# New state and output of a DeltaNet chunk: one shared PSUM bank, or one each

## The chip, the cores and the metric

The kernel runs on one core of a Trainium2 chip. A core has five engines, each with its own queue of instructions that it takes in order: TensorE (PE in the profile; its weight loads are PEld), VectorE (DVE), ScalarE (ACT), GpSimd (POOL) and SyncE (SP, which issues most DMAs here). They meet only at semaphores. TensorE writes its results into PSUM, which is divided into banks; VectorE and ScalarE read them from there. The metric is the device time of one launch in microseconds (us).

## What is computed

Two decoder layers on 1024 tokens of width 1024. Layer 0 mixes tokens with a gated DeltaNet (8 heads of 128), layer 1 with latent attention; each is followed by a dense SwiGLU network, and a conditioning vector sets shift, scale and gate of every part. The change is in the DeltaNet's recurrence, which in the reference is this scan over chunks of a head:

```python
def step(S, xs):
    q_i, k_i, w_i, u_i, a_i, gl_i = xs
    v_new = u_i - jnp.einsum("bhck,bhkv->bhcv", w_i, S)
    o_i = jnp.einsum("bhck,bhkv->bhcv", q_i, S) + jnp.einsum("bhij,bhjv->bhiv", a_i, v_new)
    S = S * gl_i[..., None, None] + jnp.einsum("bhck,bhcv->bhkv", k_i, v_new)
    return S, o_i
```

The state S (128 x 128 per head) is all that passes from one chunk to the next. The kernel takes chunks of 128 tokens, so a head has 8 (c = 0 to 7).

## The kernel before

The DeltaNet stage goes through the 8 heads one after the other (`gdn_heads`). Work of three kinds is laced into one order for TensorE: the recurrence of head h, the preparation of heads h + 1 and h + 2 (convolved keys, queries and values, decay matrices, the triangular inverse), and a stream F of projection matmuls, 128 x 512 each, for the heads to come (`take(F, n)` lets n of them go; n is 12 for heads 0 to 4, 9, 8 and 10 for heads 5, 6 and 7). In head 7 F is the output projection.

TensorE's order in this stage is the one written down. VectorE, ScalarE, GpSimd and SyncE get theirs from a scheduler, which places each instruction when it expects its inputs.

One chunk of the recurrence, by the lines of the kernel before:

- part 0: two matmuls on the state, K S (L535) and Q S (L536), into one tile `pks`. VectorE makes r from the first (L538), ScalarE makes qs from the second (L541). Then 12 matmuls of F.
- part 1: the matmul on r with the inverse U (L545); ScalarE copies it out as y (L547). Then `gdn_kv` transposes the next chunk's v and k (L515, L517) into one tile, and ScalarE reads them out as vs and kdr (L518, L522). Then, by chunk, pieces of the inverse (`gdn_merge`), L585, `gdn_kk` and `gdn_qq`.
- part 2: a tile `po` of two halves. The state's matmul (L552) fills the first half; VectorE updates S from it (L556; in chunk 0 a copy, L554). The output's matmul (L558) fills the second half; VectorE adds qs and keeps the result as `on` (L563; in chunk 0 a copy, L565). ScalarE squares and sums `on` (L567). Chunk 7 has no state update. Then pieces of `gdn_at` and `gdn_L`, 12 more matmuls of F, and the next chunk.

All these tiles have the name "d" and come from the pool `pd`, which has two buffers, one bank each, used in turn:

```python
self.pd = s2.enter_context(tc.tile_pool(name="pd", bufs=2, space=PSUM))
```

A tile may be written when all readers of the tile before it in the same bank are done. With four tiles a chunk (pks, py, the transposes, po), pks and the transposes are always in one bank, py and po in the other. The other PSUM pools are `pp` (F), `pc` (tag "c") and `pe` (tag "e"), two buffers each, eight in all.

VectorE also runs the triangular inverse of a head ahead (L454 and L456 in turn, 31 times, then L459; L470 puts it into U), the convolution (L323, three times per half; L327), weight splits (L178), the sums for the conditioning vector (L117, L119), the diagonal of K K (L391) with its scale (L393 to L401) and the matrix L (L410). ScalarE's L326 is the tanh of the convolution and waits for the third L323. The small powers `rk` and `co` are GpSimd's (L219).

Of the kernel before, what the change touches and what calls it, by code (L numbers as in the profile page):

```python
# [9 lines left out]
F32 = mybir.dt.float32  # L10
# [4 lines left out]
ALU = mybir.AluOpType  # L15
# [4 lines left out]
P = 128  # L20
# [12 lines left out]
class Trunk:  # L33
# [491 lines left out]
    def gdn_rec(self, h, c, part):  # L525

        nc, v, kq, pr = self.nc, self.nc.vector, self.kqv[h], self.pr[h]
        g, cs, cc = h * NT + c, slice(c * P, (c + 1) * P), c % 4
        if part == 0:
            self.r, self.qs = self.kv[1], None  # L530
            if c == 0:
                self.S = self.gs.tile([P, P], F32, name="S")
                return
            pks = self.pd.tile([P, 2, P], F32, name="d")
            nc.tensor.matmul(pks[:, 0], kq["KT"][:, cs], self.S, start=True, stop=True)  # L535
            nc.tensor.matmul(pks[:, 1], kq["QT"][:, cs], self.S, start=True, stop=True)  # L536
            r = self.gw.tile([P, P], F32, name="r", bufs=2)
            v.scalar_tensor_tensor(out=r, in0=pks[:, 0], scalar=pr["c2"][:, c:c + 1], in1=self.kv[1],  # L538
                                   op0=ALU.mult, op1=ALU.add)
            self.qs = self.gw.tile([P, P], F32, name="qs", bufs=2)  # L540
            nc.scalar.activation(out=self.qs, in_=pks[:, 1], func=AF.Copy, scale=self.eg[:, g:g + 1])  # L541
            self.r = r
        elif part == 1:
            py = self.pd.tile([P, P], F32, name="d")
            nc.tensor.matmul(py, pr["U"][:, c], self.r, start=True, stop=True)  # L545
            self.y = self.gw.tile([P, P], F32, name="y", bufs=2)
            nc.scalar.copy(self.y, py)  # L547
            self.kd = self.kv[0]
        else:
            po = self.pd.tile([P, 2, P], F32, name="d")  # L550
            if c < NT - 1:
                nc.tensor.matmul(po[:, 0], self.kd, self.y, start=True, stop=True)  # L552
                if c == 0:
                    v.tensor_copy(self.S, po[:, 0])  # L554
                else:
                    v.scalar_tensor_tensor(out=self.S, in0=self.S, scalar=self.egl[:, g:g + 1], in1=po[:, 0],  # L556
                                           op0=ALU.mult, op1=ALU.add)
            nc.tensor.matmul(po[:, 1], pr["at"][:, c], self.y, start=True, stop=True)  # L558
            if cc == 0:
                pr["on"] = self.gw.tile([P, 4, P], F32, name="on"), self.gs.tile([P, 4], F32, name="ss")  # L560
            on, ss = pr["on"]
            if c > 0:
                v.tensor_tensor(out=on[:, cc], in0=po[:, 1], in1=self.qs, op=ALU.add)  # L563
            else:
                v.tensor_copy(on[:, cc], po[:, 1])  # L565
            junk = self.gw.tile([P, P], BF16, name="junk2")
            nc.scalar.activation(out=junk, in_=on[:, cc], func=AF.Square, accum_out=ss[:, cc:cc + 1])  # L567
            if cc == 3:

                t1 = self.gs.tile([P, 4], F32, name="t1")  # L570
                v.tensor_scalar(out=t1, in0=pr["qq"][:, c - 3:c + 1], scalar1=EPS, scalar2=P * EPS, op0=ALU.add,
                                op1=ALU.mult)
                v.scalar_tensor_tensor(out=t1, in0=ss, scalar=1.0 / P, in1=t1, op0=ALU.mult, op1=ALU.add)
                co = self.gs.tile([P, 4], F32, name="co")
                self.rpow(co, t1)
                v.tensor_tensor(out=on, in0=on, in1=co.rearrange("p (c o) -> p c o", o=1).broadcast_to([P, 4, P]),
                                op=ALU.mult)
# [1082 lines left out]
```

## Time and profile before

| | us |
|---|---|
| median of 3 timed runs | 2702.81 (2699.43 to 2705.99) |
| the profiled execution | 2703.33 |
| its span, first to last instruction | 2701.6 |
| TensorE busy (94% of the span) | 2531.3 |
| VectorE busy (73%) | 1979.5 |
| ScalarE busy (43%) | 1171.4 |
| GpSimd busy (6%) | 154.6 |
| mean granted TensorE clock | 0.973 of full speed |

A row of the order of time gives the start, the length, the engine, the line, what is written from what, and in brackets how long the engine stood idle before it and which instruction ended that. x2 means that two instructions are merged: a fp32 matmul of this kernel runs as two. A row of the table of stretches gives for each engine the busy time and the number of instructions, then the granted clock (1.00 is full speed). The ends of matmuls are modelled, and two matmuls overlap, so a sum of TensorE's lengths is more than its time.

### The profile page before, as it was taken

How to read it: one execution, taken by the hardware profiler on the slowest of the kernel's cores; microseconds unless marked ns; L12 is line 12 of the kernel's file. 1: busy time of each engine (PE TensorE's matmuls, PEld its weight loads, DVE VectorE, ACT ScalarE, POOL GpSimd, SP SyncE). 2: the span in 40 equal slices, each digit the busy share in tenths (PEclk: the TensorE clock that was granted, in tenths of full speed). 3: DMA queues.
4: the chain of work that ended last, by engine and by line, in shares of the span. 5: the costliest groups of instructions: out<-in, count | busy, mean ns of one | idle time of the engine just before them, and what ended most of it. 6: DMA issues, size and time to landing. Idle time of an engine off the chain costs nothing.

```text
span 2701.6 us, 35351 instructions
## 1 busy us (share of the span) xinstructions
PE 2531.3 (94%) x12749; PEld 2095.8 (78%) x12749; DVE 1979.5 (73%) x3748; ACT 1171.4 (43%) x2366; POOL 154.6 (6%) x322
## 2 busy tenths in 40 slices
PE   6968898888889999999999999999989999999998
PEld 5657777776767888888888788888868888887776
DVE  5797888876755988878567866667658777774678
ACT  5535445454436523222234475555455333322443
POOL 1111111111000000000000010000000000000000
PEclk8989999999989999999999999999999999999999
DMA  6101221221155455544583622111563323325734
GB/s 221 40 24 36 79 83 56 86 82 40 40 169 194 145 164 175 165 140 160 179 293 94 216 85 65 49 46 59 170 205 100 102 97 108 103 94 198 250 101 140
DMA packets 258703, 327.60 MB, mean 121 GB/s; under 512 B 17578, under 2 KB 176448, under 8 KB 258528
## 3 DMA queue, kind: packets, MB, share of 16 engines
q1 hardware_dynamic: 235840, 284.37, 33.6%
q10 hardware_dynamic: 22688, 40.97, 4.0%
q8 instruction: 100, 1.64, 0.3%
q14 instruction: 75, 0.61, 0.1%
HBM read 247.16 MB, written 78.14 MB: 120 GB/s over the span
## 4 chain that ended last, share of the span: by engine, by line
PE 74%; DVE 14%; ACT 4%; DMA 4%; POOL 2%; issue 2%; SPq 0%; POOLq 0%; DVEq 0%; ACTq 0%
PE pd L1123 15%; PE nrm_p L202 14%; PE pd L202 9%; PE pj L202 7%; PE P L202 7%; PE pj L346 5%; PE pd L1440 3%; PE po L202 2%; DVE cacc L323 2%; PE pj L862 2%; DMA wraw<-in_ada_w_dram 2%; PE pq L202 1%; DVE X L456 1%; DVE st L454 1%; PE tp L1483 1%
## 5 line engine op out<-in xcount | busy, mean ns | idle before, releaser
L1123 PE MATMUL pd<-wlo,gh 128*128 128x512 f32 x616 | 244.1, 397 | 1.4 <-DVE wlo L178 1.0
L1123 PE MATMUL pd<-whi,gl 128*128 128x512 f32 x616 | 241.4, 393 | 1.0 <-DVE gl L178 1.0
L1123 PE MATMUL pd<-whi,gh 128*128 128x512 f32 x616 | 237.6, 395 | 3.6 <-ACT gh L177 3.3
L346 PE MATMUL pj<-hThi,whi 128*128 128x512 f32 x480 | 203.9, 425 | 0.0
L346 PE MATMUL pj<-hThi,wlo 128*128 128x512 f32 x480 | 196.5, 409 | 0.0
L346 PE MATMUL pj<-hTlo,whi 128*128 128x512 f32 x480 | 195.5, 407 | 0.0
L177 ACT CAST gh<-wraw 128x1024 fp32r<-128x1024 f32 x84 | 82.3, 979 | 247.0 <-PE pd L1123 207.8
L177 ACT CAST whi<-wraw 128x1024 fp32r<-128x1024 f32 (+3 forms) x105 | 100.8, 961 | 160.5 <-DMA wraw<-in_ffn_w_gate_dram 49.0
L1123 PEld LDWEIGHTS pd<-wlo,gh 128*128 128x128 f32 x616 | 116.5, 189 | 32.3 <-DVE wlo L178 6.9
L1123 PEld LDWEIGHTS pd<-whi,gh 128*128 128x128 f32 x616 | 116.6, 189 | 30.8 <-ACT gh L177 4.5
L178 DVE TENSOR_TENSOR gl<-wraw,gh 128x1024 fp32r<-128x1024 f32 x84 | 95.2, 1133 | 60.9 <-ACT gh L177 60.7
L1123 PEld LDWEIGHTS pd<-whi,gl 128*128 128x128 f32 x616 | 116.5, 189 | 27.0 <-DVE gl L178 1.4
L178 DVE TENSOR_TENSOR wlo<-wraw,whi 128x1024 fp32r<-128x1024 f32 (+3 forms) x105 | 116.3, 1108 | 27.7 <-ACT whi L177 26.3
L202 PE MATMUL nrm_p<-T,xrow 128*128 128x512 f32 (+1 forms) x576 | 133.7, 386 | 0.0
L202 PE MATMUL nrm_p<-T,ow_hi 128*128 128x512 f32 (+1 forms) x600 | 132.0, 368 | 0.0
L219 POOL TENSOR_TENSOR nrm_r<-nrm_r,mh 128x1 f32<-128x1 f32 x56 | 37.7, 674 | 1598.5 <-DVE nrm_r L213 1589.5
L202 PE MATMUL nrm_p<-T,ow_lo 128*128 128x512 f32 (+1 forms) x552 | 125.9, 376 | 0.0
L202 PEld LDWEIGHTS nrm_p<-T,xrow 128*128 128x128 f32 x576 | 105.1, 188 | 23.7
L202 PEld LDWEIGHTS nrm_p<-T,ow_hi 128*128 128x128 f32 x600 | 103.6, 188 | 20.7
L323 DVE SCALAR_TENSOR_TENSOR cacc<-cr,cwc,cacc 128x512 f32<-128x512 f32 x144 | 107.5, 753 | 12.9 <-ACT cacc L321 11.3
L202 PEld LDWEIGHTS nrm_p<-T,ow_lo 128*128 128x128 f32 x552 | 97.9, 188 | 20.6
L346 PEld LDWEIGHTS pj<-hThi,wlo 128*128 128x128 f32 x480 | 94.8, 197 | 21.5
(544 smaller groups left out, 6405.7 us busy)
## 6 DMA issues: line engine op xcount, KB each, us to landing
wraw<-in_ada_w_dram SPq DMA_DIRECT2D x80, 512.0 KB, 4.1
wraw<-in_ffn_w_gate_dram SPq DMA_DIRECT2D x44, 512.0 KB, 4.2
wraw<-in_ffn_w_up_dram SPq DMA_DIRECT2D x44, 512.0 KB, 4.7
gd_S<-sx ACTq DMA_DIRECT2D x88, 256.0 KB, 2.6
B<-in_ffn_w_down_dram SPq DMA_DIRECT2D x40, 512.0 KB, 6.9
wraw<-gd_S SPq DMA_DIRECT2D x40, 512.0 KB, 4.6
gd_A<-co ACTq DMA_DIRECT2D x66, 256.0 KB, 2.2
wraw<-in_gdn_w_in_dram SPq DMA_DIRECT2D x32, 512.0 KB, 4.2
```

The source lines that it names most:

```text
L177: nc.scalar.copy(hi, raw)
L178: nc.vector.tensor_tensor(out=lo, in0=raw, in1=hi.bitcast(F32), op=ALU.subtract)
L202: nc.tensor.matmul(out, l, r, start=(i == 0), stop=(i == len(seq) - 1))
L219: self.nc.gpsimd.tensor_tensor(out=out, in0=in_, in1=self.mh[:, 0:in_.shape[1]], op=ALU.pow)
L323: nc.vector.scalar_tensor_tensor(out=acc, in0=cr[:, j:j + 512], scalar=self.cw[:, j, ch:ch + 1], in1=acc, op0=ALU.mult, op1=ALU.add)
L346: self.nc.tensor.matmul(pj, l[:, kt], r[:, kt, sl], start=(kt == j == 0), stop=(kt == KT - 1 and j == 2))
L454: v.tensor_tensor(out=t[:, 0:n], in0=Lr[:, j, j + 1:32].rearrange("p (i o) -> p i o", o=1).broadcast_to([P, n, 8]), in1=X[:, j:j + 1].broa ...
L456: v.tensor_tensor(out=X[:, j + 1:32], in0=X[:, j + 1:32], in1=t[:, 0:n], op=ALU.subtract)
L862: nc.tensor.matmul(po, l[:, i], r[:, ns], start=(i == j == 0), stop=(i == 3 and j == 2))
L1123: nc.tensor.matmul(acc[t], x[:, j, ts], y[:, j], start=(j0 + j == 0 and k == 0), stop=(j0 + j == NJ - 1 and k == 2))
L1440: nc.tensor.matmul(sc[:, 0:nm], q[:, ts], k[:, cs], start=(i == 0), stop=(i == 4 and not last))
L1483: nc.tensor.transpose(pt[:, kt - k0], pes[qi][:, kt * P:(kt + 1) * P], self.ident)
```

## The change

The tile `po` of two halves becomes two tiles of 128 columns. `psn`, for the new state, is taken only in chunks 0 to 6; `po`, for the output, in every chunk. Both come from the same pool of two banks, so a chunk now takes five tiles instead of four: pks, py, the transposes, psn, po. Each chunk therefore starts on the other bank than the one before it, psn lies in the bank of py, and po in the bank of the transposes. The arithmetic and the number of instructions are the same. All lines from 558 on have a number higher by one.

```diff
--- before.py
+++ after.py
@@ -547,22 +547,23 @@
             nc.scalar.copy(self.y, py)
             self.kd = self.kv[0]
         else:
-            po = self.pd.tile([P, 2, P], F32, name="d")
             if c < NT - 1:
-                nc.tensor.matmul(po[:, 0], self.kd, self.y, start=True, stop=True)
+                psn = self.pd.tile([P, P], F32, name="d")
+                nc.tensor.matmul(psn, self.kd, self.y, start=True, stop=True)
                 if c == 0:
-                    v.tensor_copy(self.S, po[:, 0])
+                    v.tensor_copy(self.S, psn)
                 else:
-                    v.scalar_tensor_tensor(out=self.S, in0=self.S, scalar=self.egl[:, g:g + 1], in1=po[:, 0],
+                    v.scalar_tensor_tensor(out=self.S, in0=self.S, scalar=self.egl[:, g:g + 1], in1=psn,
                                            op0=ALU.mult, op1=ALU.add)
-            nc.tensor.matmul(po[:, 1], pr["at"][:, c], self.y, start=True, stop=True)
+            po = self.pd.tile([P, P], F32, name="d")
+            nc.tensor.matmul(po, pr["at"][:, c], self.y, start=True, stop=True)
             if cc == 0:
                 pr["on"] = self.gw.tile([P, 4, P], F32, name="on"), self.gs.tile([P, 4], F32, name="ss")
             on, ss = pr["on"]
             if c > 0:
-                v.tensor_tensor(out=on[:, cc], in0=po[:, 1], in1=self.qs, op=ALU.add)
+                v.tensor_tensor(out=on[:, cc], in0=po, in1=self.qs, op=ALU.add)
             else:
-                v.tensor_copy(on[:, cc], po[:, 1])
+                v.tensor_copy(on[:, cc], po)
             junk = self.gw.tile([P, P], BF16, name="junk2")
             nc.scalar.activation(out=junk, in_=on[:, cc], func=AF.Square, accum_out=ss[:, cc:cc + 1])
             if cc == 3:
```

TensorE has the same instructions in the same order; what differs is which engine's semaphore a matmul waits for. The rows are from head 6, chunk 6, where no matmul of F lies between the chunks. Names in brackets are the engines waited for.

Before:

```order
L496 MATMUL e<-U,L 64x64 [waits PE_49]
L496 MATMUL e<-U,L 64x64 x3
L498 MATMUL e<-ident,U 64x64 [waits PE_49]
L498 MATMUL e<-ident,U 64x64 x3
L552 MATMUL d<-y,kdr 128x128 [waits Activation_49]
L558 MATMUL d<-y,at 128x128 [waits DVE_49]
L535 MATMUL d<-S,KT 128x128 [waits Activation_49]
L536 MATMUL d<-S,QT 128x128
L545 MATMUL d<-r,U 128x128 [waits DVE_49]
```

Now:

```order
L496 MATMUL e<-U,L 64x64 [waits PE_49]
L496 MATMUL e<-U,L 64x64 x3
L498 MATMUL e<-ident,U 64x64 [waits PE_49]
L498 MATMUL e<-ident,U 64x64 x3
L552 MATMUL d<-y,kdr 128x128 [waits Activation_49]
L559 MATMUL d<-y,at 128x128 [waits Activation_49]
L535 MATMUL d<-S,KT 128x128 [waits DVE_49]
L536 MATMUL d<-S,QT 128x128
L545 MATMUL d<-r,U 128x128 [waits DVE_49]
```

The output's matmul (L558, now L559) waited for VectorE and waits for ScalarE now; the first matmul on the state (L535) waited for ScalarE and waits for VectorE now. So it is in every chunk.

VectorE's order, from the state's update of head 2, chunk 3, into chunk 4 (junk is the diagonal of K K, t and co the output's norm, b and c scales).

Before:

```order
L556 SCALAR_TENSOR_TENSOR S<-S,eg_947,d 128x128
L391 SCALAR_TENSOR_TENSOR junk,kd<-c,ident 128x128 x2
L563 TENSOR_TENSOR on<-d,qs 128x128
L391 SCALAR_TENSOR_TENSOR junk,kd<-c,ident 128x128
L393 TENSOR_SCALAR kd<-kd 128x4
L398 TENSOR_TENSOR rkb<-rk,beta 128x4
L573 SCALAR_TENSOR_TENSOR t_3715<-ss,t_3715 128x4
L400 TENSOR_TENSOR b_3705<-rk,rkb 128x4
L119 SCALAR_TENSOR_TENSOR wraw<-wraw,cact 128x1024
L401 SCALAR_TENSOR_TENSOR c_3685<-b_3705,eg_947 128x4
L576 TENSOR_TENSOR on<-on,co 128x512
L410 SCALAR_TENSOR_TENSOR L<-c,b_3705,dec 128x128 x4
```

Now:

```order
L556 SCALAR_TENSOR_TENSOR S<-S,eg_947,d 128x128
L391 SCALAR_TENSOR_TENSOR junk,kd<-c,ident 128x128
L564 TENSOR_TENSOR on<-d,qs 128x128
L391 SCALAR_TENSOR_TENSOR junk,kd<-c,ident 128x128 x2
L574 SCALAR_TENSOR_TENSOR t_3733<-ss,t_3733 128x4
L393 TENSOR_SCALAR kd<-kd 128x4
L577 TENSOR_TENSOR on<-on,co 128x512
L398 TENSOR_TENSOR rkb<-rk,beta 128x4
L538 SCALAR_TENSOR_TENSOR r<-d,c_1971,vs 128x128
L400 TENSOR_TENSOR b_3722<-rk,rkb 128x4
L178 TENSOR_TENSOR wlo<-wraw,whi 128x1024
L401 SCALAR_TENSOR_TENSOR c_3702<-b_3722,eg_947 128x4
```

r (L538) came right behind the L410 of the first list and now stands ahead of them; the step L119 has gone elsewhere; `on` stands one place nearer to S. In most chunks `on` follows S at once now.

ScalarE's order in head 1, chunk 1.

Before:

```order
L541 ACTIVATE qs<-d,eg_947 128x128
L547 COPY y<-d 128x128
L518 ACTIVATE vs<-d,rkb 128x128
L522 ACTIVATE kdr<-d,eg_947 128x128
L326 ACTIVATE KT<-cacc 128x512
L367 ACTIVATE decT<-c 128x512
```

Now:

```order
L541 ACTIVATE qs<-d,eg_947 128x128
L547 COPY y<-d 128x128
L518 ACTIVATE vs<-d,rkb 128x128
L326 ACTIVATE KT<-cacc 128x512
L522 ACTIVATE kdr<-d,eg_947 128x128
L367 ACTIVATE decT<-c 128x512
```

The tanh L326 has moved ahead of kdr. In chunk 1 of heads 0, 2, 3 and 4 it stood ahead of vs and now stands between vs and kdr.

## Rows read from the trace of the kernel before

**Rows 1.** The page's first line.

```profile
span 2701.6 us, 35351 instructions
```

**Rows 2.** Stretches: range, length, busy PE, PEld, DVE, ACT, POOL, clock, DMA share, GB/s.

```profile
194.64:266.87 72.23, 64.53 (x366) 54.03 (x366) 53.25 (x137) 37.23 (x101) 9.88 (x19) 0.98 0.10 31
266.87:611.14 344.27, 306.78 (x1675) 255.71 (x1673) 280.71 (x708) 166.52 (x441) 49.57 (x80) 0.95 0.26 77
611.14:813.50 202.36, 173.89 (x935) 143.48 (x934) 127.17 (x318) 85.09 (x239) 19.05 (x27) 0.92 0.26 85
sum 618.86, PE 545.20 PEld 453.22 DVE 461.13 ACT 288.84 POOL 78.49; mean PE 181.73 PEld 151.07 DVE 153.71 ACT 96.28 POOL 26.16
```

**Rows 3.** Waits of PE, 190 to 815 us: total us, times, longest.

```profile
PE d L558 <- DVE S L556: 50.6, 48, 2.2
PE d L558 <- DVE S L554: 7.7, 8, 1.2
...
PE d L545 <- DVE r L538: 3.1, 6, 0.9
```

**Rows 4.** Order of time, head 2, chunk 5.

```profile
416.62 0.49 PE L552 MATMUL d<-y,kdr 128*128 128x128 f32 x2
416.86 0.36 ACT L522 ACTIVATE kdr<-d,eg 128x128 f32<-128x128 f32 x1
...
418.11 0.57 DVE L488 TENSOR_SCALAR U<-e 32x128 f32<-32x128 f32 x2
...
418.72 0.35 DVE L556 SCALAR_TENSOR_TENSOR S<-S,eg,d 128x128 f32<-128x128 f32 x1
...
419.12 0.49 PE L558 MATMUL d<-y,at 128*128 128x128 f32 x2 [2.00 <-DVE S L556]
```

**Rows 5.** Order of time, head 2, chunk 2.

```profile
382.81 0.36 ACT L522 ACTIVATE kdr<-d,eg 128x128 f32<-128x128 f32 x1
...
383.39 0.49 PE L552 MATMUL d<-y,kdr 128*128 128x128 f32 x2
...
383.91 0.35 DVE L556 SCALAR_TENSOR_TENSOR S<-S,eg,d 128x128 f32<-128x128 f32 x1 [0.20 <-PE d L552]
...
384.31 0.49 PE L558 MATMUL d<-y,at 128*128 128x128 f32 x2 [0.44 <-DVE S L556]
...
384.84 0.29 DVE L563 TENSOR_TENSOR on<-d,qs 128x128 f32<-128x128 f32 x1
```

**Rows 6.** Chain that ended last: two runs of F behind head 2's chunk 5.

```profile
419.61 4.35 PE pj L346 x12
424.40 2.76 PE pj L346 x12
```

**Rows 7.** Order of time, head 0, chunk 1.

```profile
203.59 0.44 PE L552 MATMUL d<-y,kdr 128*128 128x128 f32 x2
204.05 0.63 ACT L326 ACTIVATE KT<-cacc 128x512 f32<-128x512 f32 x1 [1.05 <-DVE cacc L323]
...
204.84 0.36 ACT L522 ACTIVATE kdr<-d,eg 128x128 f32<-128x128 f32 x1
```

**Rows 8.** Order of time, head 1, chunk 4: the matmul on r.

```profile
317.96 0.49 PE L545 MATMUL d<-r,U 128*128 128x128 f32 x2 [0.17 <-DVE r L538]
```

**Rows 9.** Order of time, chunk 3: first and last of six, heads 0 and 5.

```profile
225.50 0.49 PE L558 MATMUL d<-y,at 128*128 128x128 f32 x2 [0.44 <-DVE S L556]
...
652.26 0.49 PE L558 MATMUL d<-y,at 128*128 128x128 f32 x2 [0.51 <-DVE S L556]
```

**Rows 10.** Stretches: chunk 1 of heads 0, 1, 3, 5, 6, the sum.

```profile
sum 60.92, PE 48.63 PEld 39.52 DVE 54.85 ACT 21.62 POOL 13.22; mean PE 9.73 PEld 7.90 DVE 10.97 ACT 4.32 POOL 2.64
```

**Rows 11.** Stretch of 2 us behind head 2's chunk 5, columns as in rows 2.

```profile
420.00:422.00 2.00, 2.00 (x7) 1.61 (x6) 1.97 (x6) 1.38 (x7) 0.00 (x0) 0.58 0.00 0
```

**Rows 12.** Waits of PE in heads 1 to 4, 266.87 to 611.14 us.

```profile
PE d L558 <- DVE S L556: 28.9, 24, 2.2
PE d L558 <- DVE S L554: 4.3, 4, 1.2
```

## The prediction

> **What bounds the kernel now.** I read the page first: the profiled execution spans 2701.6 us [rows 1] and took 2703.33 us, so 1.7 us lie around the span; the median of the three timed runs, 2702.81 us, is half a microsecond less. TensorE is busy most of the span, so only idle time of TensorE or a slow TensorE clock can be won anywhere. Second, the view by stretches, cut at the output matmuls (L558) of each head's last chunk: the recurrence that the change touches runs from 194.64 to 813.50 us. In its 618.9 us TensorE is busy 545.2 and VectorE 461.1 [rows 2], so TensorE idles 73.7 us, a ninth of the stage, while VectorE is not full either (75%; 82% in heads 1 to 4). Third, TensorE's waits of that stage: two rows, both L558 waiting for VectorE's write of the state S (L556, and L554 in chunk 0), hold 50.6 + 7.7 = 58.3 us in 56 waits, four fifths of the idle time; the wait for r (L545) is 3.1 us [rows 3].
>
> The order of time then shows why. In head 2, chunk 5, the state's matmul L552 starts at 416.62; VectorE is still in older work (L488 until 418.68), does S at 418.72, and only at 419.12 does L558 start, 2.00 us idle behind it [rows 4]. L558 needs y, which L552 had already, and not S. It waits because S's update reads the bank that L558 writes. Where VectorE is free at once, as in head 2, chunk 2, the wait is still 0.44 us [rows 5]. So the least is 0.44 and the mean 58.3 / 56 = 1.04 us.
>
> **What the change removes.** The output gets a tile of its own, so L558 waits for ScalarE alone and the wait for S moves to the next chunk's first matmul (L535), as the instruction orders show. Between the two stand 12 matmuls of the projection stream (9, 8 and 10 in heads 5 to 7), some 2.76 us [rows 6]. S ends 2.45 us after L552 in rows 4, one of the longest waits, and L535 cannot come before 0.49 + 0.3 + 2.76 = 3.5 us after it; only where the stream has run out (head 6, chunks 6 and 7) does nothing lie between. I count the wait at L535 as hidden, and if that cover were gone the 0.44 us least of rows 5 would come back. Removed: **58.3 us**.
>
> **What it adds, in five terms.**
>
> (a) A new wait. The ring of two banks now turns five times a chunk, and the output lands in the bank of the next chunk's transposed k and v, whose readers are ScalarE's vs and kdr (L518, L522). In rows 5's chunk kdr was done at 383.17, before L552; in chunk 5 kdr ends at 416.86 + 0.36 = 417.22, against 417.11 for the end of L552 [rows 4], a wait of 0.1 to 0.2. I take that for chunks 5 and 7, 14 in all: 2 us. In head 0, chunk 1, the tanh L326 stands ahead of kdr and waits for VectorE's convolution; kdr ends at 205.20, L552 at 204.03 [rows 7]: 1.2 us. Head 1 gets that order too. Together 2 + 2 x 1.2, rounded up to 5; bounds 0 and 12 (2.0 us, as in rows 4, in chunk 1 of five heads, and the 2). Queued behind the waiting L558 is the stream, and nothing but `on` waits for L558 itself.
>
> (b) r becomes late. VectorE does not become faster, so where it was behind, its next result is late next. In chunk 4 of head 1, the matmul on r (L545) already waits 0.17 us for it [rows 8]: no slack is left. What is saved at S in chunk 3 (0.44 in head 0 to 0.51 in head 5, six waits of heads 0 to 5, 6.8 in sum [rows 9]) and in chunk 0 (7.7 [rows 3]) can thus come back as a wait for r. Bounds: 0, since the new VectorE order puts r ahead of the four L410 and of a step for the conditioning vector (L119), and 14.5. I take the middle, 7.
>
> (c) Chunks in which VectorE has more to do than TensorE. In chunk 1 of heads 0, 1, 3, 5 and 6 VectorE is busy 54.85 us, TensorE 48.63 [rows 10]; without the wait these five are paced by VectorE, so 6.2 us stay, taken as 6. Bounds 0 (the new order spreads the substitution steps of L454 and L456 into chunks 2 and 3) and 12 (they then crowd those chunks as well).
>
> (d) VectorE's `on` (L563) now stands right behind S. It cannot start before L558 has run: L558 starts 0.49 after L552 at the earliest, `on` followed L558 by 0.53, so 1.02 after L552, while S ends 0.87 after it [rows 5]. VectorE idles 0.15 x 56 = 8.4 us, hidden in its 158 us of idle time. Bounds 0 and 8; I take 2.
>
> (e) TensorE's clock. After the 2.00 us wait of chunk 5 the granted clock fell to 0.58 of full in the stretch 420 to 422 [rows 11], that is, to the lower of its two levels (1.2 GHz) for most of it, and the next 12 stream matmuls took 4.35 instead of 2.76 us [rows 6]. It fell so in chunk 5 or 6 of each of heads 0 to 4. With the wait of chunk 5 cut to 0.2 us I expect those five falls gone: 5 x 1.59 = 8 us back. Bounds: 0, and 14 (nine falls that come within 2 us of a wait for S of 1.4 us or more).
>
> The Trainium skill's page "TensorE: Matmul & The Clock Gate", section "A second HAM failure mode: psum-queue depth-cycling", says that small idles between groups of matmuls that cycle through PSUM banks are enough to make the clock swing; the fall in rows 11 behind a 2 us wait agrees. Taken as the rule for the whole stage it would give back every slow stretch, which is the third rival below.
>
> Sum: -58.3 + 5 + 7 + 6 + 2 - 8 = -46.3 us. On the profiled execution's own 2703.3 us that is **2657 us**, all of it inside the recurrence (619 to some 573 us). The rest keeps its instructions: TensorE's order is the same to the last row, and only VectorE's, ScalarE's, GpSimdE's and SyncE's move, within this stage.
>
> **Rivals.**
> 1. VectorE takes over the pace in heads 1 to 4, where it is busy 280.7 of 344.3 us [rows 2]; the work it used to do between S and `on` now queues elsewhere, and TensorE waits for r instead of S. Then those heads keep most of their 344 us and only heads 0 and 5 to 7 gain, by their own waits for S (58.3 less the 33.2 of heads 1 to 4 [rows 12] is 25, some 20 after (a)): 2683. Half of it gives 2670. For it: [rows 8, 10]. Against it: VectorE idles 63 us in these heads, much of it waiting for TensorE.
> 2. Slower: kdr. ScalarE's tanh (L326) or its copies before kdr make L558 wait for kdr in every chunk as long as in rows 7, 1.2 us. 56 x 1.2 = 67 instead of 58.3, with the 2 us of chunk 7: 2714. It decides from a mean lateness of 1.04 us on. For it: the new ScalarE order puts L326 between vs and kdr in chunk 1 of several heads, and VectorE now stands still behind `on` while L558 waits, which delays the very convolution that L326 needs. Against it: in chunks like that of rows 5 kdr is done before L552 starts.
> 3. The clock comes back whole and VectorE keeps up: terms (b) to (d) fall away and some 25 us of TensorE's time at the lower level return (the stage's granted clock is 0.92 to 0.98, which costs 2% of 72 + 5% of 344 + 8% of 202 = 35 us [rows 2]; 10 of it lie in heads 6 and 7 behind other waits). -58.3 + 5 - 25 = -78: 2625. By the Trainium skill's section above this is the case to expect.
> 4. The change doesn't do what it says: the bank was not what held L558, or the chain through VectorE sets each chunk's length and L535 or L545 waits for all that L558 waited: 2703. Against it: in chunks like that of rows 5 VectorE itself had waited 0.20 us for TensorE before S, so there the chain runs through TensorE.
>
> **How the numbers follow.** Chances: forecast 0.52 (2645 to 2668), VectorE's pace 0.24 (2668 to 2692), the clock 0.10 (2620 to 2645), nothing 0.06, slower 0.08. A measurement of this kernel can tell 0.2%, 5.4 us, from no change. Faster is 0.52 + 0.24 + 0.10 = 0.86, same 0.06, slower 0.08. The best ends of the terms give 2703 - 58 - 14 = 2631, the worst with the clock unchanged 2703 - 58 + 12 + 14 + 12 + 8 = 2691. The range 2634 to 2690 leaves out a little of the third rival and the last two.
>
> **What the profile after would show.** Right: L559 (L558 before) waits for no VectorE instruction, and for ScalarE under 8 us in all; TensorE's idle time between the same marks falls from 74 to some 30 us; L545's wait for r grows from 3 to about 10 us; VectorE's share rises to about 80%; the falls of the clock behind chunk 5 are gone. (a) is wrong if the wait for kdr is over 12 us, (b) and (c) if the wait for r is over 20, (e) if the stage's granted clock does not rise. The whole is wrong if the stage shortens by less than 15 us, or if the time outside it moves by more than 5.

## The result and the profile after

The changed kernel takes 2635.27 us in the median of four runs (2630.46 to 2645.68), the kernel before 2701.12 beside it: a ratio of 0.976, with a 95% interval from 0.9724 to 0.9796. Forecast were 2657 us in a range from 2634 to 2690. The gain is 66 us and not 46. The measured time lies inside the range, 1.3 us from its lower end, and in the band of the third rival (2620 to 2645, chance 0.10), not in the forecast's own (2645 to 2668, 0.52).

The profiled execution is 72 us shorter than that of [rows 1]; the page counts the same work on each engine as before (12749 matmuls, 3748 instructions on VectorE, 2366 on ScalarE). First line of the page:

```profile
span 2629.7 us, 35337 instructions
```

The same three stretches as in [rows 2], cut at the output matmuls (now L559) of the same chunks:

```profile
195.41:259.56 64.15, 61.83 (x368) 52.49 (x366) 50.88 (x138) 38.06 (x102) 10.03 (x19) 1.00 0.13 37
259.56:560.74 301.18, 287.84 (x1674) 241.92 (x1672) 266.08 (x700) 167.51 (x441) 49.31 (x80) 0.99 0.30 88
560.74:742.01 181.27, 165.84 (x935) 137.88 (x933) 127.59 (x328) 85.74 (x239) 20.13 (x27) 0.94 0.29 95
sum 546.60, PE 515.50 PEld 432.28 DVE 444.54 ACT 291.30 POOL 79.47; mean PE 171.84 PEld 144.09 DVE 148.18 ACT 97.10 POOL 26.49
```

There are three readings. The stage went from 618.86 to 546.60 us, and the time outside it stayed (2082.7 before, 2083.1 now). TensorE's idle time (stretch less PE) went from 73.7 to 31.1. And TensorE's own busy time went from 545.2 to 515.5 with the same instructions, mostly because the granted clock rose from 0.98, 0.95 and 0.92 to 1.00, 0.99 and 0.94. A reader who looks at idle time alone misses the third reading, and it is nearly 30 of the 72 us.

The waits of TensorE (total us, times, longest), in answer to [rows 3]:

```profile
PE d L515 <- ACT qs L541: 9.6, 8, 2.7
PE d L545 <- DVE r L538: 6.5, 9, 2.2
PE d L559 <- ACT kdr L522: 3.6, 6, 1.6
PE c L586 <- DVE on L577: 2.7, 2, 1.8
...
PE d L535 <- DVE S L556: 0.2, 1, 0.2
```

The two waits for S are gone, and no other took their size. Head 2, chunk 5 again, in order of time, in answer to [rows 4]:

```profile
389.86 0.36 ACT L522 ACTIVATE kdr<-d,eg 128x128 f32<-128x128 f32 x1
...
390.68 0.39 PE L552 MATMUL d<-y,kdr 128*128 128x128 f32 x2
390.90 0.39 PE L559 MATMUL d<-y,at 128*128 128x128 f32 x2
...
393.35 0.35 DVE L556 SCALAR_TENSOR_TENSOR S<-S,eg,d 128x128 f32<-128x128 f32 x1
...
393.89 0.38 PE L535 MATMUL d<-S,KT 128*128 128x128 f32 x2
```

VectorE is now even later with S (2.67 us behind L552; before, 2.10; in the mean of the stage 1.50 and 1.10), and it costs nothing: L559 follows L552 at once, the stream follows L559, and S is done 0.2 us before L535 asks for it. The clock behind it, in answer to [rows 11], stays whole:

```profile
390.00:392.00 2.00, 2.00 (x16) 1.88 (x16) 2.00 (x7) 1.55 (x4) 0.00 (x0) 1.00 0.67 161
392.00:394.00 2.00, 2.00 (x11) 1.57 (x11) 1.91 (x7) 1.91 (x7) 0.10 (x1) 1.00 0.59 178
```

Read in pieces of half a microsecond, the granted clock of the stage is at the lower level for some 75 us in 15 stretches before, for some 24 us in 3 after.

### The profile page after: what moved, and what is told of

It is laid out like the page before. It is cut to its first block, busy times and chain, and to the rows that moved or that the text cites. A ratio compares the mean times of both kernels' runs of the same rounds, so it can differ in the third digit from the quotient of the medians.

```text
span 2629.7 us, 35337 instructions
## 1 busy us (share of the span) xinstructions
PE 2503.7 (95%) x12749; PEld 2077.0 (79%) x12749; DVE 1962.3 (75%) x3748; ACT 1175.0 (45%) x2366; POOL 155.5 (6%) x322
## 4 chain that ended last, share of the span: by engine, by line
PE 75%; DVE 12%; ACT 5%; DMA 4%; issue 2%; POOL 2%; SPq 0%; POOLq 0%; DVEq 0%; ACTq 0%
PE pd L1124 14%; PE nrm_p L202 14%; PE pd L202 10%; PE pj L202 7%; PE P L202 7%; PE pj L346 5%; PE pd L1441 3%; PE po L202 2%; DVE cacc L323 2%; PE pj L863 2%; PE pq L202 1%; DVE X L456 1%; PE tp L1484 1%; DVE st L454 1%; DMA wraw<-in_ada_w_dram 1%
## 5 line engine op out<-in xcount | busy, mean ns | idle before, releaser
L346 PE MATMUL pj<-hThi,whi 128*128 128x512 f32 x480 | 198.9, 414 | 0.0
L346 PE MATMUL pj<-hThi,wlo 128*128 128x512 f32 x480 | 191.8, 400 | 0.0
L346 PE MATMUL pj<-hTlo,whi 128*128 128x512 f32 x480 | 190.7, 397 | 0.0
L323 DVE SCALAR_TENSOR_TENSOR cacc<-cr,cwc,cacc 128x512 f32<-128x512 f32 x144 | 107.9, 755 | 10.2 <-ACT cacc L321 9.4
L346 PEld LDWEIGHTS pj<-hThi,wlo 128*128 128x128 f32 x480 | 91.8, 191 | 20.4
```

The source lines that it names most:

```text
L323: nc.vector.scalar_tensor_tensor(out=acc, in0=cr[:, j:j + 512], scalar=self.cw[:, j, ch:ch + 1], in1=acc, op0=ALU.mult, op1=ALU.add)
L346: self.nc.tensor.matmul(pj, l[:, kt], r[:, kt, sl], start=(kt == j == 0), stop=(kt == KT - 1 and j == 2))
```

## The experiments

Each kernel was timed in 4 to 12 runs beside runs of the kernel before. For each run the span and its mean granted clock are known, so I use two sums: the **time at full clock**, span x clock, and the time **lost to the clock**, the rest. Over 48 runs of the kernel before the first is 2625 with a standard deviation of some 3 us, while the second goes from 67 to 92 (mean 82): nearly all its scatter is the clock. The table has the means of both. From the one trace of each kernel come TensorE's idle time in the stage, its idles of 1 us and more, and the number of stretches at the lower clock. The letters of the theories hold within one experiment only.

| kernel | median us | ratio to before, 95% | full clock | lost | idle | of 1 us | low |
|---|---|---|---|---|---|---|---|
| before | 2701 to 2714 | 1 | 2625 | 82 | 73.7 | 27 | 15 |
| changed, again | 2637.8 | 0.973 (0.9704 to 0.9755) | 2577 | 58 | 31.0 | 8 | 4 |
| c1_busy_wait | 2695.6 | 0.994 (0.9919 to 0.996) | 2641 | 53 | 37.1 | 11 | 5 |
| e1_back_to_back | 2650.4 | 0.9778 (0.9751 to 0.9805) | 2577 | 70 | 35.6 | 10 | 7 |
| p3_before_priority | 2688.2 | 0.9912 (0.989 to 0.9934) | 2616 | 69 | 62.1 | 26 | 9 |
| e2_fill | 2705.4 | 0.9989 (0.9973 to 1.0005) | 2615 | 89 | 64.9 | 25 | 15 |
| e5_split_c5 | 2694.3 | 0.9953 (0.9932 to 0.9974) | 2623 | 70 | 69.1 | 26 | 10 |
| e4_shared_c5 | 2649.2 | 0.9772 (0.9746 to 0.9798) | 2582 | 63 | 35.9 | 13 | 8 |
| e9_dve_extra | 2648.8 | 0.9762 (0.9736 to 0.9789) | 2581 | 64 | 33.5 | 13 | 6 |
| e8_kv_first | 2638.7 | 0.9744 (0.9721 to 0.9767) | 2583 | 57 | 38.8 | 11 | 5 |
| e8b_kv_first_after | 2654.6 | 0.9782 (0.9756 to 0.9808) | 2583 | 68 | 40.4 | 14 | 8 |
| b1_merge_first | 2641.6 | 0.9732 (0.9711 to 0.9753) | 2579 | 58 | 33.4 | 10 | 4 |
| p1_priority | 2642.0 | 0.9742 (0.9719 to 0.9764) | 2576 | 63 | 29.6 | 10 | 9 |

**How much of the gain is the clock.** The changed kernel, unedited.

> The changed kernel again, beside the next three, for how much of its gain is the clock. Each run gives a span and a mean granted clock; span x clock is the time at full clock, and the rest what the clock cost. By the profiled runs: kernel before 2701.6 x 0.973 = 2629 and 73 us lost; changed kernel 2629.7 x 0.981 = 2580 and 50 us lost. Theory A (the clock's share of the gain holds from run to run): 2580 and 45 to 55 us lost in the mean, against some 75 to 80 before. Theory E (the one profiled run was a lucky one): 2580, but 65 us lost or more, so the clock gives back about the 8 us that the prediction had, and the gain is 50 to 60 us.

2577 at full clock, 48 less than before; 58 lost (53 to 66), 24 less than before's mean. The gain is two thirds time at full clock and one third clock, and this holds from run to run. That is nearer to theory A than to E: the profiled execution of the changed kernel lost less than the mean, but so did that of the kernel before (50 and 73).

**Is it TensorE's idling that costs the clock?**

```diff
+            if c < NT - 1:
+                dm = self.pd.tile([P, P], F32, name="d")
             po = self.pd.tile([P, 2, P], F32, name="d")
...
                 nc.tensor.matmul(po[:, 0], self.kd, self.y, start=True, stop=True)
+                for _ in range(4):
+                    nc.tensor.matmul(dm, self.ident, self.ident, start=True, stop=True)
```

> The kernel before, one bank for both results as there, with four extra 128x128 matmuls (identity by identity, into a fifth tile of the ring that nobody reads; about 0.9 us) between the state's matmul and the output's, where TensorE stood idle. Nothing is saved by it: waits under 0.9 us get longer by 12 us in sum, and the output's matmul may wait some 3 us for kdr as in the changed kernel. It asks whether the clock's part of the gain comes from TensorE being busy there. Theory A (the clock falls behind long idles of TensorE, whatever ends them): of the 22 idles of 1.5 us and more in the stage some 6 stay, and the loss to the clock (span x (1 - granted clock), a mean of 80 to 84 us in the kernel before, 58 in the changed one) falls to 60 to 65, while the time at full clock grows from 2625 to about 2640: 2700 to 2705 us. Theory H (the clock's part comes from the separate bank, or from the VectorE order that goes with it): the loss stays at 78 to 85, so 2718 to 2725.

State and output still share a bank, S still makes the output's matmul (now L562) wait, and the work has grown by four matmuls in 56 chunks. The two largest groups of waits of its trace, and the stage's stretch (columns as in [rows 2]):

```profile
PE d L562 <- DVE S L560: 15.7, 19, 1.5
PE d L515 <- ACT qs L541: 5.0, 5, 2.7
```

```profile
202.07:810.51 608.44, 571.34 (x3411) 486.53 (x3411) 462.04 (x1161) 288.95 (x779) 77.23 (x126) 0.98 0.25 76
```

The time at full clock grew by 16 us, as expected, and the loss to the clock fell from 82 to 53, so the kernel with useless work added is faster than the one without, by 0.4 to 0.8%. This is theory A, and the loss fell further than I expected: the clock's part of the gain comes back when TensorE is kept busy at this place, without a bank of its own for the output. The scheduler also moved some of VectorE's instructions, but not in S's favour: S starts 1.18 us behind the state's matmul in the mean, before 1.10. One rival is left to the next run: c1 takes five tiles of the ring a chunk, as the changed kernel does. The stream's matmuls show the clock too; before, c1 and changed, one of the three forms of L346 in the stage (line, engine, operation, tile, count, busy us, mean ns, idle before):

```profile
L346 PE MATMUL pj<-hThi,whi 128*128 128x512 f32 x396 | 169.6, 428 | 0.0
```

```profile
L346 PE MATMUL pj<-hThi,whi 128*128 128x512 f32 x396 | 163.1, 412 | 0.0
```

```profile
L346 PE MATMUL pj<-hThi,whi 128*128 128x512 f32 x396 | 163.5, 413 | 0.0
```

The Trainium skill's page "TensorE: Matmul & The Clock Gate", section "A second HAM failure mode: psum-queue depth-cycling", tells of a bf16 kernel in which small idles between groups of matmuls were frequent enough to make the clock swing; the traces agree, with 15 low stretches before and 5 here. The Trainium skill's page "PSUM — Partial Sum Buffer", section "Summary: rules for kernel authors", says, for reading PSUM while a matmul runs, to target a different bank or to guard by bank with semaphores. The kernel before has the guard, and its price there is the 58.3 us of waits; the change takes the other bank. The next run tries a third way: no matmul into the bank comes behind the read.

**Is a second bank needed?** The matmul moved, nothing else:

```diff
                 nc.tensor.matmul(po[:, 0], self.kd, self.y, start=True, stop=True)
+            nc.tensor.matmul(po[:, 1], pr["at"][:, c], self.y, start=True, stop=True)
+            if c < NT - 1:
                 if c == 0:
...
-            nc.tensor.matmul(po[:, 1], pr["at"][:, c], self.y, start=True, stop=True)
```

> The kernel before with one edit: the two matmuls are issued back to back into the two halves of the one tile, and only then comes the update of S. The bank stays shared and the ring keeps four tiles a chunk, so there is no wait for kdr. Theory A (only the wait of the output's matmul between the two cost time): all 58.3 us of waits go without a second bank, the clock comes back as in the changed kernel, and kdr's 3.6 us are spared: 2628 to 2638 us, about the changed kernel's 2635 or a few us less; TensorE's idle time in the stage 26 to 32 us. Theory B (the bank itself is needed, because S now reads a bank that TensorE has only just finished and comes later by one matmul, 0.25 us, in 56 chunks): r and the chain through VectorE get later, idle time 40 to 50 us and half of the clock's gain, 2650 to 2670.

At full clock it is the changed kernel to the microsecond (2577). The waits for S are nearly gone with one bank:

```profile
PE d L535 <- DVE S L558: 1.8, 3, 0.9
```

So a second bank is not needed to remove them: it was enough that no reader of the bank stood between the two matmuls. It lost 12 us more to the clock, which puts the median at the lower end of B's range; but B's reason, an S made late in every chunk, would show at full clock, and does not. It takes four tiles of the ring a chunk, as the kernel before does, and still loses 12 us less than that one to the clock. The longest wait of its trace, which the changed kernel doesn't have, is for r, and it is one of order: in head 3, chunk 6 VectorE was given three steps of the convolution (L323) ahead of r, and the first waited for ScalarE:

```profile
486.93 0.75 DVE L323 SCALAR_TENSOR_TENSOR cacc<-cr,cwc,cacc 128x512 f32<-128x512 f32 x1 [1.55 <-ACT cacc L321]
...
489.89 0.35 DVE L538 SCALAR_TENSOR_TENSOR r<-d,c,vs 128x128 f32<-128x128 f32 x1
...
490.29 0.80 PE L545 MATMUL d<-r,U 128*128 128x128 f32 x2 [4.95 <-DVE r L538]
```

TensorE stood 4.95 us there. Whether that and the clock stretch around it make up all of the 12 us is not shown.

**Did the new order of VectorE bring the gain?** The kernel before, with r, S, on, qs, y, vs and kdr each under `with self.tc.high_priority():`.

> The kernel before, one bank as there, with only the order of VectorE and ScalarE changed: r, S, on, qs, y, vs and kdr go ahead of other work that is ready at the same time. Rival I (the gain of the change came with the new order of VectorE and not from the bank): S comes earlier, most of the 33.7 us of waits above the least of 0.44 go, and the clock with them: 2660 to 2675. Theory A: the wait is the bank's and its least, 56 x 0.44 = 25 us, cannot go; and an instruction that is under way is not interrupted, so that only part of the rest goes: 0 to 25 us, 2680 to 2705.

Waits for S (L562 updates S, L560 is the copy of chunk 0):

```profile
PE d L564 <- DVE S L562: 38.7, 48, 2.2
PE d L564 <- DVE S L560: 7.3, 8, 1.1
```

They fell from 58.3 to 46.0, the kernel by 0.7 to 1.1%: theory A's range. So an order that puts these steps first is worth about a third of the gain, 9 us at full clock and 13 lost to the clock; the rest needs the wait itself gone. In the changed kernel S is not earlier but later, so its own new order is not what removed the wait.

**Can work hide the wait in one bank?** A chunk has two runs of twelve stream matmuls, one behind part 0 (between L536 and L545) and one behind part 2 (ahead of the next L535). Six of the first run moved to between the two matmuls of part 2; chunk 0, which has no L545 that waits for r, got its six from chunk 7.

```diff
+            fill()
             nc.tensor.matmul(po[:, 1], pr["at"][:, c], self.y, start=True, stop=True)
...
-                take(F, n)
+                take(F, n - 6 if c else n)
...
-                self.gdn_rec(h, c, 2)
+                self.gdn_rec(h, c, 2, lambda: take(F, 6 if c < NT - 1 else 0))
```

> The kernel before with one edit: 6 of the 12 stream matmuls of a chunk (1.38 us) are issued between the state's matmul and the output's, in one bank as before. Theory A (the wait is TensorE's idle time and nothing else): each wait is covered up to 1.38 us; of the 58.3 us 9.8 are left (the parts above 1.38), and as TensorE is kept busy most of the half-clock stretches go too, some 20 of the 30 us: 2630 to 2650. If the clock's 30 us came from the separate bank or the new VectorE order and not from TensorE being kept busy, they stay: 2655 to 2670. Theory B (the chain through VectorE sets the chunk): the time before, 2690 to 2705.

Theory A as I had written it failed, and theory B has the time. Its trace has these waits:

```profile
PE d L545 <- DVE r L538: 44.2, 26, 3.8
...
PE d L559 <- DVE S L556: 4.5, 5, 1.9
```

The waits for S went from 58.3 to 5.4, and the waits for r from 3.1 to 44.2. The first run of twelve was what covered VectorE's lateness at r; half of it, taken from there to cover S, uncovered r, and nothing was won. So VectorE was late for TensorE all along, and the one place without cover paid. The change works because it takes nothing from r: S is now asked for at L535 only, behind the second run of twelve, which stood there before as well.

**One chunk alone, both ways.** In the changed kernel chunk 5 shares a tile again; in the kernel before chunk 5 alone gets two. `one` is `c == 5` in the first, `c != 5` in the second:

```diff
+            if one:
+                pair = self.pd.tile([P, 2, P], F32, name="d")
+                psn, po = pair[:, 0], pair[:, 1]
...
+                if not one:
+                    psn = self.pd.tile([P, P], F32, name="d")
...
+            if not one:
+                po = self.pd.tile([P, P], F32, name="d")
```

> The changed kernel, but in chunk 5 of every head the two results share one tile again as before. The waits of chunk 5 come back: 2.0 us in heads 0 to 4 and 0.4 to 0.9 in the rest, 12 us. Theory C (a fall of the clock belongs to one wait of 2 us, as the prediction had it): the five falls behind chunk 5 come back as well, 5 x 1.6 = 8 us, so 2655 and five more half-clock stretches than the changed kernel's three. Theory D (the clock falls where several idle stretches follow each other over a chunk or two; one alone does not do it): 12 us and none or one of the falls, 2645 to 2649.

> The mirror of the run before: the kernel before, with two tiles in chunk 5 alone. 12 us of waits go. Theory C: the falls behind chunk 5 of heads 0 to 4 go with them, 8 us: 2681, ten half-clock stretches left of 15. Theory D: the clock falls somewhere else in the same heads, behind the waits that are left, or goes on falling: 2686 to 2691, with 12 to 15 stretches.

With chunk 5 shared, its waits came back, 13.3 us, and those behind it shrank:

```profile
PE d L565 <- DVE S L561: 13.3, 8, 2.7
PE d L557 <- ACT y L547: 5.4, 9, 1.4
PE d L515 <- ACT qs L541: 3.4, 2, 2.7
...
PE d L545 <- DVE r L538: 2.8, 4, 1.2
```

Idle time rose by 5 us only. Behind or in the wait of chunk 5 the clock is low in four of heads 0 to 4 and there are 8 low stretches instead of 3 or 4, as theory C has it, though not by the length of the wait: in head 1 a wait of 0.44 us is followed by a fall, in head 3 one of 2.25 us is not. The loss of 5 us at full clock and about 5 to the clock is nearer to D's size. With chunk 5 split, its wait is gone, but that of chunk 6 of the same head, 0.44 us in the kernel before, is not what it was (head 1, chunks 5 and 6):

```profile
325.42 0.49 PE L565 MATMUL d<-y,at 128*128 128x128 f32 x2 [0.16 <-ACT kdr L522]
...
335.63 0.49 PE L565 MATMUL d<-y,at 128*128 128x128 f32 x2 [1.69 <-DVE S L561]
```

In heads 0 to 4 it is 1.46 to 1.70. VectorE's backlog was only handed on to the next chunk that waits for it: the mechanism of term (b). So the time at full clock fell by 2 us and not by 12; the loss to the clock fell by 12. There are 10 low stretches, as theory C has it, though three of them stand at chunk 6's wait now, which is D's reading. In both runs D is nearer in the total and C in the number of falls, and neither had the time at full clock right.

**How near is VectorE to the pace?** In the changed kernel, behind each `on`:

```diff
+            jx = self.gw.tile([P, P], BF16, name="junk")
+            for _ in range(2):
+                v.tensor_tensor(out=jx, in0=self.ident, in1=self.ident, op=ALU.add)
```

> The changed kernel with two more additions of 128x128 on VectorE in each chunk, whose result nobody reads: 2 x 0.25 us x 64 = 32 us of VectorE's time. It asks how near VectorE is to setting the pace (the prediction's first rival and its terms b and c). Slack (VectorE idles 100 of 547 us in the stage, and 12 stream matmuls cover its lateness at S and at r): 0 to 6 us slower. Pace: in heads 1 to 4, where it is busy 86% of the time, its lateness reaches TensorE: the wait for r grows from 6 to 20 us or more, and the clock falls more often: 15 to 35 us slower.

VectorE got some 37 us of work more (128 additions, 0.29 us each), which the scheduler spread from 166.0 to 685.2 us; the time at full clock rose by 4 us and the loss by 5, between the two cases. The wait for r grew from 6.5 to 8.1 us, not to 20: VectorE doesn't set the pace, but its slack isn't free.

**Four tries at what is left.** Two move the transposes L515 and L517 ahead of L545, so that they don't wait for qs (`gdn_kv` called before part 1; in one bank with the matmuls back to back, and in the changed kernel).

> One tile for both results, their matmuls back to back, and the transposes of the next chunk's v and k (L515, L517) issued ahead of the matmul on r (L545) instead of behind it; the tile of the transposes then lies in the bank of the chunk's results and no longer in that of pks, whose reader qs they wait for (9 us of TensorE's idle time in the profiles of the changed kernel and of the back-to-back one, with half-clock stretches behind several of these waits). Theory F (that wait is of the same kind as the one for S: a bank's reader, with no data in it): 9 us of idle time and 5 to 10 us of the clock go: 15 us under the back-to-back kernel, 2630 to 2640. Theory G (ScalarE is late with everything, so the matmul on r or the one on y waits as long): no change, 2645 to 2655. Slower, if vs and kdr now stand ahead of y on ScalarE and make it late by 0.7 us in many chunks: 2665 or more.

> The same move of the transposes in the changed kernel, two tiles for the results. Theory F: 10 to 20 us under the changed kernel, 2615 to 2625. Theory G: 2632 to 2638. Slower, if y gets late: 2650 or more.

The wait went to the next matmul: in the second of them L545 waits 16.1 us for qs and once 4.9 us for the tanh (L326), and L551 waits 8.1 for y. The first has theory F's median, but by the clock: at full clock it is 6 us above the back-to-back kernel, so the wait was not won. The second comes out as the slower case, with y late.

The third puts the merge ahead of the transposes in chunk 6:

```diff
+                if c == 6:
+                    if h < H - 1:
+                        take(m0)
+                    if h + 2 < H:
+                        self.gdn_qq(h + 2, 1)
                 if c < NT - 1:
                     self.gdn_kv(h, c + 1)
...
```

> The changed kernel with useful work put into its largest remaining wait: in chunk 6 of each head the matmuls of the inverse's merge (L496, L498) and of the next Q's transposes (L419), some 1.3 us, are issued ahead of the transposes L515, which wait for qs there (2.15, 0.93, 0.95, 0.94 and 1.15 us in heads 1 to 5, 2.67 in head 6; 9.6 in all) and not behind them. Theory A (an idle time filled with work is won, and what it cost in clock behind it comes back): 5 to 7 us of idle time and 5 to 10 us of the clock (the loss of 58 falls to 50): 2622 to 2630. Rival (ScalarE is late with y as well, and the matmul on y then waits for as long): 2632 to 2642.

There is no change, which is the rival's case, and the names of the waits say why: the wait for qs fell from 9.6 to 3.0 us, but vs and y come late now, and r's grew from 6.5 to 9.3 with one wait of 5.1.

```profile
PE d L559 <- ACT vs L518: 5.9, 6, 2.1
...
PE d L515 <- ACT qs L541: 3.0, 3, 1.7
PE d L552 <- ACT y L547: 3.0, 5, 1.5
```

The fourth gives the changed kernel the preference of p3_before_priority.

> The changed kernel with that same preference for r, S, on, qs, y, vs and kdr on VectorE and ScalarE. What is left of TensorE's idle time in the changed kernel is mostly one of these being late: qs 9.6, r 6.5, kdr 3.6 us. Theory J (they are late because the scheduler places casts, the convolution and the steps of the conditioning vector ahead of them): 10 to 15 us of idle time go and 5 to 10 us of the clock: 2615 to 2625. Theory K (they are late because VectorE and ScalarE are in the middle of a long instruction, or because what is moved behind them is waited for next, the inverse, the diagonal, oT): 2630 to 2645, with other names in the waits.

Theory K holds: r's wait fell from 6.5 to 2.6 us, and waits for U (L470) and L (L410), 4.1 us each, took its place. No version clearly beat the changed kernel.

## Why the prediction was right, and where it was off

The wait and the direction were right, and so was the mechanism of the gain at full clock. The size of the clock's part was wrong by a factor of three, and the terms that give time back are right in their sum more by luck than by their mechanisms.

- **The wait removed (-58.3): right, and whole.** L559 waits for no VectorE instruction; e1 shows that S's read between two matmuls into one bank was what held it, since with the two issued in a row, in the same bank, the wait goes. L535's wait for S is 0.2 us in all, as the 12 matmuls of [rows 6] had let expect.
- **(a), kdr: 5 forecast, 3.6 measured**, in chunk 1 of heads 0, 1 and 6 and in chunk 5 of heads 0, 1 and 3; chunk 7, which I had counted too, has none. In head 0, chunk 1, in answer to [rows 7]:

```profile
204.26 0.44 PE L552 MATMUL d<-y,kdr 128*128 128x128 f32 x2
205.35 0.63 ACT L326 ACTIVATE KT<-cacc 128x512 f32<-128x512 f32 x1 [1.37 <-DVE cacc L323]
...
205.89 0.35 ACT L522 ACTIVATE kdr<-d,eg 128x128 f32<-128x128 f32 x1
...
206.29 0.49 PE L559 MATMUL d<-y,at 128*128 128x128 f32 x2 [1.59 <-ACT kdr L522]
```

- **(b), r: 7 forecast, 3.4 measured** (3.1 to 6.5). The sign is right in sum, but not the place: I expected the waits in chunks 4 and 1, and chunk 4's fell from 2.3 to 1.4 us while chunk 1 has none. What came is in chunk 3 (2.5 us) and in chunks 5 to 7. The stream's cover at r was worth more than I gave it, as e2 shows by taking half of it away.
- **(c), chunk 1: 6 forecast, about 0.2 measured.** In answer to [rows 10], the sum of the same five stretches:

```profile
sum 54.21, PE 47.59 PEld 38.38 DVE 51.09 ACT 20.97 POOL 10.87; mean PE 9.52 PEld 7.68 DVE 10.22 ACT 4.19 POOL 2.17
```

  There are 6.6 us of idle time, of which 2.7 are kdr's, already in (a). The other 3.9 are waits for oT, for a piece of the inverse and for decT. Before, these chunks had 12.3 us of idle time, of which the waits for S were 8.6; the other 3.7 were waits for a piece of the inverse:

```profile
PE e L159 <- DVE U L488: 3.7, 2, 2.0
```

  These were never part of the 58.3 and would have stayed in any case, so they did not belong among my 6.2 of new idle time. The new order also took 3.8 us of VectorE's work out of this chunk.
- **(d), on: 2 forecast, none measured.** VectorE waits 0.5 us for L559 in the whole stage. S is so late that `on` nearly always finds its matmul done.
- **Not forecast:** the wait for qs went from 4.7 to 9.6, and 3.4 us of waits for oT came. The give-backs together are 31.1 - (73.7 - 58.3) = 15.7 us (14.9 if one leaves out the first wait for S, 0.8 us, which lies ahead of the first cut); forecast were 20. Of these (a) to (d) are 7.2 and qs and oT 8.3, so the sum came near by luck.
- **(e), the clock: the term that failed.** "With the wait of chunk 5 cut to 0.2 us I expect those five falls gone: 5 x 1.59 = 8 us back." All five are gone, and seven others. In the profiled pair the stage lost 37.5 us to the clock and loses 11.9; over all runs the difference is 24 us, three times the 8 and above the bound of 14. I had tied falls to a wait of 1.4 us or more close by, one by one. That count was too small: c1, which puts some work into every wait for S, brings 29 us back. Which share each single wait had is not shown.
- **The rivals.** The third rival had the clock's size (25), and (b) to (d) shrank to 3.6 us, nearly as it said; what it lacked are the waits that came for qs and oT. With the measured terms the sum is -58.3 + 15.7 - 25.6 = -68. The 4 us more of the profiled pair are TensorE's busy time at full clock, 507.7 to 503.6: L558 beside its wait takes 0.49 us [rows 4], L559 right behind L552 0.39. VectorE's pace did not set in (VectorE's share of the stage is 81%), though e2, where r's wait grew to 44.2 us, shows how little cover it takes away to bring it. Kdr as a slowdown took 3.6 us instead of 67. The fourth rival, that the bank was not what held L558, is answered by the wait that is gone.

## What to carry to other kernels

Before a wait is removed, ask which engine is late, and where else TensorE will meet it. Here one run of twelve stream matmuls covers r and another covers S once S is asked for behind it; when six of the first were moved ahead of S's wait, they covered S and uncovered r. Where waits of about a microsecond recur in a stage with a granted clock under 1, count a good part of the clock's loss there as their cost (here 25.6 of 37.5 us), and measure it by span x clock over several runs. In this kernel two matmuls into one bank needed no second bank to lose the wait, if they were issued back to back, ahead of the first reader; that version had the same time at full clock and lost 12 us more to the clock.

## What was not expected of the hardware

- Useless matmuls in TensorE's waits made the kernel faster: 16 us more at full clock, 29 less lost.
- A single long wait doesn't always bring the clock down. In the changed kernel L515 waits 2.15 us in head 1, and the stretches around it keep 1.00:

```profile
324.97 0.33 PE L515 MATMUL d<-ident,VT 128*128 128x128 f32 x1 [2.15 <-ACT qs L541]
```

```profile
322.00:324.00 2.00, 0.82 (x5) 0.55 (x3) 1.21 (x3) 1.95 (x4) 0.00 (x0) 1.00 0.00 0
324.00:326.00 2.00, 1.03 (x12) 0.85 (x13) 1.93 (x3) 1.50 (x6) 0.00 (x0) 1.00 0.00 0
```

  When the same kernel was run again, the clock fell at the end of the same wait:

```profile
333.35 0.48 PE L515 MATMUL d<-ident,VT 128*128 128x128 f32 x1 [2.18 <-ACT qs L541]
```

```profile
332.00:334.00 2.00, 0.65 (x3) 0.42 (x4) 1.54 (x3) 1.59 (x5) 0.00 (x0) 0.79 0.00 0
334.00:336.00 2.00, 2.00 (x15) 1.71 (x15) 2.00 (x6) 0.97 (x3) 0.00 (x0) 0.50 0.61 160
```

  So the pattern of waits alone does not decide which idle brings a fall, and what does stays open: p1_priority idles least of all (29.6 us) and has 9 low stretches, where the changed kernel has 3 or 4.
- The scatter between runs of one kernel is the clock's: span x clock repeats to some 3 us, while the loss of the kernel before goes from 67 to 92.
